# A decoder layer on one core: where the woven substitution steps stand beside VectorE's softmax operations

## The chip, the core and the metric

One core of a Trainium2 chip runs the whole kernel in one launch. The metric is the device time in microseconds (us) of one execution, as the median of several runs. The engines are TensorE (PE in the profile, its weight loads PEld), VectorE (DVE), ScalarE (ACT), GpSimd (POOL) and SyncE (SP, which issues most DMAs). Each has its own queue and works through it in order; they meet through semaphores.

## The reference

One layer over 2048 tokens of width 1024, all in float32. A normalised input goes through one projection into two groups of heads. Eight attention heads look back over a sliding window of 128 tokens, with a learned sink per head, whose logit takes part in the maximum and the sum of the softmax:

```python
s = s - slopes * dist                      # ALiBi
s = jnp.where(valid, s, NEG_INF)
m = jnp.maximum(jnp.max(s, axis=-1, keepdims=True), sink)
p = jnp.exp(s - m)
denom = jnp.sum(p, axis=-1, keepdims=True) + jnp.exp(sink - m)
o = einsum(p / denom, v)
```

Eight RWKV-7 heads update a 64x64 state per token; `S = S*w + (S a) b + v k`, read out as `S r`. Both groups share an output projection, and a gated MLP with a short causal convolution and a last normalisation follow.

## The kernel before

The first stage (to about 1150 us) does projection, attention and RWKV; then come the output projection and the MLP, which the change does not touch.

The first stage works in 16 units: four blocks of 512 tokens by four indices j, each with two RWKV heads and two attention heads. Loop `n` runs three units at once: projection and preparation of unit n+2, the chunk matrices of unit n+1, the recurrence (`chain`, eight chunks of 64 tokens) and the attention of unit n. The code issues instructions for all of them in one written order: a list `dense` of projection pieces, a list `other` of steps with positions from the table `Q`, and `defer`, which puts a step on a list to be issued some estimated microseconds later. `in_order` pins the order of TensorE, ScalarE and VectorE as issued; GpSimd's and SP's order is pinned in the prologue only.

For RWKV the inverse of a unit triangular matrix is needed per chunk. `px` makes the products, VectorE masks them into XB, `inv_in` sends the 32x32 diagonal blocks through DRAM (dL) and back as LL, laid out so that all blocks of a unit are solved at once on 128 partitions. `subst` is that forward substitution: 31 steps of two VectorE operations, `mul` (Mt = M x LL) and `add` (M = M + Mt), each needing the one before. `inv_out` sends M through DRAM (dT) to TT, and `merge0` (a transpose on VectorE) to `merge2` complete the inverse, which the next unit's `chain` needs.

The 62 operations of `subst` are not issued at once. They go onto the list `woven`. Each VectorE operation issued through `ordered` (line 120; its operations show as L124) calls `weave`, which issues one operation from the list behind it. `subst_to`, at 30 positions along the unit, issues what is still due by then, and `inv_out` stands behind the last.

Attention of a unit (`t_attn`) has four softmaxes, over q2 and g. `scores` issues the matmuls into pS and four VectorE operations: two fused reductions (the scaled scores plus bias, with the maximum into m; CUSTOM in the profile, each with a small read of its accumulator), the negation of m into nm, and es = nm + sink. `go1` follows later, with ScalarE's exponentials of es and P, which also sum; `go2` later still: sm + es, its reciprocal, and two scalings of P. `ptr` transposes P on TensorE, ScalarE copies it (pth), VectorE takes the rest (ptl), and `pv` multiplies by V into pO. In the profile the small operations show as m<-m, the scalings as P<-P. All of these VectorE operations go through `ordered`, so each is followed by a woven step while the list holds any.

Of the kernel before, what the change touches and what calls it, by code (L numbers as in the profile page):

```python
# [13 lines left out]
ALU = mybir.AluOpType  # L14
# [4 lines left out]
P = 128  # L19
# [64 lines left out]
def hybrid_trunk_kernel(  # L84
# [7 lines left out]
    order = {"on": True}  # L92
# [10 lines left out]
    def mm(**kw):  # L103
        in_order("pe", nc.tensor.matmul(**kw))  # L104

    def tr_(**kw):
        in_order("pe", nc.tensor.transpose(**kw))

    def act(*args, **kw):
        in_order("act", nc.scalar.activation(*args, **kw))  # L110
# [3 lines left out]
    def weave():  # L114
        if woven and not order.get("busy"):
            order["busy"] = True
            woven.pop(0)()
            order["busy"] = False

    def ordered(name):  # L120
        f = getattr(nc.vector, name)

        def go(*args, **kw):
            in_order("dve", f(*args, **kw))  # L124
            weave()
        return go
# [16 lines left out]
    tt = ordered("tensor_tensor")  # L143
    stt = ordered("scalar_tensor_tensor")
    tsc = ordered("tensor_scalar")
    vcopy = ordered("tensor_copy")
    recip = ordered("reciprocal")
    scan = ordered("tensor_tensor_scan")
    ttr = ordered("tensor_tensor_reduce")
# [3 lines left out]
    def f32(ap):  # L153
        return ap.bitcast(F32)
# [14 lines left out]
    def dma(**kw):  # L169
        i = nc.sync.dma_start(**kw)  # L170
        if order.get("prologue", True):
            in_order("sp", i)
# [16 lines left out]
    def mm3(ps, passes, first=True, last=True, **kw):  # L189
        n = len(passes)  # L190
        for i, (lh, ll, rh, rl) in enumerate(passes):
            mm(out=ps, lhsT=lh, rhs=rh, start=first and i == 0, stop=False, **kw)
            mm(out=ps, lhsT=lh, rhs=rl, start=False, stop=False, **kw)
            mm(out=ps, lhsT=ll, rhs=rh, start=False, stop=last and i == n - 1, **kw)


    with ExitStack() as A:
# [80 lines left out]
        sinkb = acon.tile([P, 8], F32, name="sinkb")  # L278
# [7 lines left out]
        bias = acon.tile([P, 256], mybir.dt.bfloat16, name="bias")  # L286
# [112 lines left out]
        def defer(us, fn, key=None):  # L399
            clk["n"] += 1  # L400
            todo.append((clk["t"] + us, clk["n"], fn, key))
            todo.sort(key=lambda d: d[:2])
# [6 lines left out]
        def need(key):  # L409
            while any(d[3] == key for d in todo):  # L410
                todo.pop(0)[2]()
# [328 lines left out]
        def t_x(F, n):  # L740
# [101 lines left out]
            def subst_to(i):  # L842
                def go():
                    while len(woven) > 2 * (30 - i):
                        weave()
                return go
# [152 lines left out]
        def t_attn(n):  # L999
            b, j = divmod(n, NPAIR)  # L1000
            S = {}

            def w0_(q2, e):
                return P if (b == 0 and q2 == 0 and e == 0) else 0

            def scores(q2, g):
                def go():
                    assert H["kb"] == b
                    need(f"q{j}_{b}")
                    need(f"kv_{b}")  # L1010
                    qg = H[b, j, "q"][g]
                    if q2 == 0 and g == 0:
                        S["o"] = ap_.tile([P, BLK], F32, tag="oT", name=f"oT_{b}_{j}")
                    u = f"{b}_{j}_{q2}_{g}"
                    hd = 4 * g + j
                    gs = hs[g]
                    Pm = S[q2, g] = ap_.tile([P, 2, 256], F32, tag="P", name=f"P_{u}", bufs=2)
                    col = ap_.tile([P, 4, 2], F32, tag="m", name=f"m_{u}", bufs=2)
                    m, nm, es, sm = (col[:, i] for i in range(4))
                    pS = ps_at.tile([P, 2, 256], F32, tag="at", name=f"pS_{u}")  # L1020
                    for e in range(2):
                        qb = 2 * q2 + e
                        w0 = w0_(q2, e)
                        kks = slice(qb + w0 // P, qb + 2)
                        qs = slice(qb * P, (qb + 1) * P)
                        mm(out=pS[:, e, w0:], lhsT=qg[:, qs], rhs=kTh[:, g, kks].rearrange("p n t -> p (n t)"),
                           start=True, stop=False)
                        mm(out=pS[:, e, w0:], lhsT=qg[:, qs], rhs=kTl[:, g, kks].rearrange("p n t -> p (n t)"),
                           start=False, stop=True)
                    for e in range(2):  # L1030
                        w0 = w0_(q2, e)
                        ttr(out=Pm[:, e, w0:], in0=pS[:, e, w0:], in1=bias[:, w0:],
                                                       scale=2.0 ** -(hd + 1), scalar=sinkb[:, hd:hd + 1], op0=ALU.add,
                                                       op1=ALU.max, accum_out=m[:, e:e + 1])
                    tsc(out=nm, in0=m, scalar1=-1.0, scalar2=None, op0=ALU.mult)
                    tt(out=es, in0=nm, in1=sinkb[:, hd:hd + 1].broadcast_to([P, 2]), op=ALU.add)

                    def go1():
                        act(es, es, AF.Exp)
                        for e in range(2):  # L1040
                            w0 = w0_(q2, e)
                            act(Pm[:, e, w0:], Pm[:, e, w0:], AF.Exp, bias=nm[:, e:e + 1], accum_out=sm[:, e:e + 1])
                        defer(Q["p2"], go2, f"p_{u}")

                    def go2():
                        tt(out=sm, in0=sm, in1=es, op=ALU.add)
                        recip(out=sm, in_=sm)
                        for e in range(2):
                            w0 = w0_(q2, e)
                            tsc(out=Pm[:, e, w0:], in0=Pm[:, e, w0:], scalar1=sm[:, e:e + 1], scalar2=None, op0=ALU.mult)  # L1050
                    defer(Q["p1"], go1, f"p_{u}")
                return go

            def ptr(q2, g):
                def go():
                    u = f"{b}_{j}_{q2}_{g}"
                    e0 = 1 if (b == 0 and q2 == 0) else 0
                    need(f"p_{u}")
                    need(f"p_{u}")
                    Pm = S[q2, g]  # L1060
                    pT = ps_at.tile([P, 4, P], F32, tag="at", name=f"pT_{u}")
                    for i in range(e0, 4):
                        tr_(out=pT[:, i], in_=Pm[:, i // 2, (i % 2) * P:(i % 2 + 1) * P], identity=ident)
                    th = S["th", g] = ap_.tile([P, 4, P], F32R, tag="pth", name=f"pth_{u}")
                    tl = S["tl", g] = ap_.tile([P, 4, P], F32R, tag="ptl", name=f"ptl_{u}")
                    act(th[:, e0:], pT[:, e0:], AF.Copy)
                    defer(Q["tl"], lambda: tt(out=tl[:, e0:], in0=pT[:, e0:], in1=f32(th[:, e0:]), op=ALU.subtract), f"t_{u}")
                return go

            def pv(q2, g):  # L1070
                def go():
                    u = f"{b}_{j}_{q2}_{g}"
                    e0 = 1 if (b == 0 and q2 == 0) else 0
                    assert H["vb"] == b
                    need(f"t_{u}")
                    th, tl = S["th", g], S["tl", g]
                    gs = hs[g]
                    pO = ps_at.tile([P, 2, P], F32, tag="at", name=f"pO_{u}")
                    for e in range(2):
                        qb = 2 * q2 + e  # L1080
                        mm3(pO[0:64, e], [(vth[:, qb + kb, gs], vtl[:, qb + kb, gs], th[:, 2 * e + kb], tl[:, 2 * e + kb])
                                          for kb in range(e0 if e == 0 else 0, 2)])
                    act(S["o"][gs, q2 * 256:(q2 + 1) * 256], pO[0:64].rearrange("p e q -> p (e q)"), AF.Copy)
                    if q2 == 1:
                        r0 = 64 * (4 * g + j)
                        dma(out=catT[r0:r0 + 64, b * BLK:(b + 1) * BLK], in_=S["o"][gs])
                return go

            return scores, ptr, pv
# [769 lines left out]
```

## Time and profile before

| | |
|---|---|
| median of 3 runs | 2682.14 us (2678.06 to 2682.83) |
| profiled execution | 2676.94 us |
| its span | 2675.2 us |
| busy: TensorE, VectorE, ScalarE, GpSimd | 94%, 65%, 49%, 55% |
| mean granted clock of TensorE | 0.976 |

The profile is that of one execution. Times in a timeline are from the start of its span. Busy time is what an engine's instructions took; a timeline's bracket gives idle time of the engine in front of an instruction and what released it. Durations on VectorE overlap a little: an instruction can start before the one in front of it has ended, so what a sequence costs is read from start to start.

### The profile page before, as it was taken

What the parts mean: (1) busy time and instruction counts of PE and PEld (TensorE: products, weight loads), DVE (VectorE), ACT (ScalarE), POOL (GpSimd) and SP (SyncE); (2) the same over time, 40 slices, a digit from 0 to 9 for tenths busy, and PEclk for the clock granted to TensorE, in tenths of its full rate; (3) what the DMA queues carried; (4) which work ended last, traced back from release to release, by engine and by line L of the source; (5) the groups of instructions that cost most, each with busy time, mean ns of one, the idle gap of its engine ahead of it and who ended that gap; (6) DMA issues with size and microseconds to landing.
All of it is one profiled execution on the core that took longest, in us unless ns stands there. A gap on an engine that the chain in (4) does not pass through costs nothing.

```text
span 2675.2 us, 42264 instructions
## 1 busy us (share of the span) xinstructions
PE 2524.3 (94%) x15211; PEld 1983.2 (74%) x15211; DVE 1733.0 (65%) x3216; ACT 1302.5 (49%) x2769; POOL 1469.3 (55%) x1364
## 2 busy tenths in 40 slices
PE   7899999999999989998989999999999999999997
PEld 5666666766667666777868787887888888888886
DVE  6578777777677746753757776767676765453336
ACT  4356655665556555544633433455333343343343
POOL 6434443444344433421747867767666665464598
PEclk9899999999999989999999999999999999999999
DMA  4222222222223222336664345455233336743354
GB/s 125 65 69 74 74 74 74 72 62 78 66 59 97 64 66 59 94 114 194 201 186 130 130 138 179 137 164 179 87 106 103 118 95 234 243 150 101 103 166 164
DMA packets 333108, 313.94 MB, mean 117 GB/s; under 512 B 102576, under 2 KB 254274, under 8 KB 332898
## 3 DMA queue, kind: packets, MB, share of 16 engines
q1 hardware_dynamic: 332290, 310.71, 38.3%
q8 instruction: 119, 1.95, 0.3%
q14 instruction: 91, 0.75, 0.1%
q10 hardware_dynamic: 608, 0.53, 0.1%
HBM read 229.26 MB, written 81.92 MB: 116 GB/s over the span
## 4 chain that ended last, share of the span: by engine, by line
PE 60%; DVE 18%; DMA 8%; ACT 5%; issue 4%; POOL 4%; SPq 1%; POOLq 0%; ACTq 0%; DVEq 0%
PE d L104 14%; PE q_g L104 13%; PE q_u L104 13%; DVE M L124 4%; DVE Mt L124 4%; PE pin_q L104 3%; DMA LL<-dL 3%; PE poa L104 2%; PE px L104 2%; PE po L104 2%; DVE P L124 2%; PE pc L104 2%; PE pin_k L104 1%; PE ph L104 1%; PE pO L104 1%
## 5 line engine op out<-in xcount | busy, mean ns | idle before, releaser
L1262 POOL TENSOR_TENSOR ul_u<-s_u,uh_u 128x512 fp32r<-128x512 f32 x154 | 214.2, 1398 | 144.3 <-ACT uh_u L110 141.1
L1262 POOL TENSOR_TENSOR ul_a<-sa,uh_a 128x512 fp32r<-128x512 f32 x154 | 210.3, 1373 | 139.7 <-ACT uh_a L110 137.7
L104 PE MATMUL q_u<-h2h,uh_u 128*128 128x512 f32 x616 | 241.3, 392 | 10.7 <-DVE u_u L1497 8.0
L1262 POOL TENSOR_TENSOR ul_g<-s_g,uh_g 128x512 fp32r<-128x512 f32 x154 | 215.9, 1410 | 59.8 <-ACT uh_g L110 57.8
L104 PE MATMUL q_g<-h2h,uh_g 128*128 128x512 f32 x616 | 241.3, 392 | 4.7 <-DVE u_g L1497 3.6
L104 PE MATMUL q_u<-h2h,ul_u 128*128 128x512 f32 x616 | 240.3, 390 | 0.4 <-POOL ul_u L1262 0.4
L104 PE MATMUL q_g<-h2l,uh_g 128*128 128x512 f32 x616 | 240.6, 391 | 0.0
L104 PE MATMUL q_g<-h2h,ul_g 128*128 128x512 f32 x616 | 240.3, 391 | 0.0
L104 PE MATMUL q_u<-h2l,uh_u 128*128 128x512 f32 x616 | 240.3, 390 | 0.0
L104 PE MATMUL d<-ul_b,uh_a 128*128 128x512 f32 x616 | 232.6, 390 | 1.8 <-DVE ul_b L1494 1.8
L104 PE MATMUL d<-uh_b,ul_a 128*128 128x512 f32 x616 | 229.4, 389 | 0.0
L110 ACT ACTIVATE uh_a<-sa 128x512 fp32r<-128x512 f32 x154 | 97.1, 631 | 228.3 <-PE d L104 127.6
L104 PE MATMUL d<-uh_b,uh_a 128*128 128x512 f32 x616 | 205.9, 389 | 0.0
L110 ACT ACTIVATE uh_u<-s_u 128x512 fp32r<-128x512 f32 x154 | 95.7, 628 | 208.9 <-DVE s_u L1494 93.7
L110 ACT ACTIVATE uh_g<-s_g 128x512 fp32r<-128x512 f32 x154 | 95.2, 629 | 207.5 <-PE q_u L104 112.7
L124 DVE TENSOR_TENSOR Mt<-M,LL 128x60 f32<-128x60 f32 (+24 forms) x496 | 159.1, 321 | 42.0 <-DMA LL<-dL 33.7
L1494 DVE TENSOR_TENSOR ul_b<-wd,uh_b 128x512 fp32r<-128x512 f32 x55 | 68.6, 1248 | 156.1 <-ACT uh_b L110 150.1
L124 DVE SCALAR_TENSOR_TENSOR cc<-g,fcst,cc 128x1024 f32<-128x1024 f32 x88 | 147.3, 1688 | 29.5 <-ACT cc L110 28.8
L124 DVE TENSOR_TENSOR M<-M,Mt 128x60 f32<-128x60 f32 (+24 forms) x496 | 156.2, 315 | 10.8
L104 PEld LDWEIGHTS q_u<-h2h,uh_u 128*128 128x128 f32 x616 | 116.0, 188 | 38.0 <-DVE u_u L1497 7.5
L104 PEld LDWEIGHTS q_g<-h2h,uh_g 128*128 128x128 f32 x616 | 116.3, 189 | 30.6 <-DVE u_g L1497 4.0
L104 PEld LDWEIGHTS d<-ul_b,uh_a 128*128 128x128 f32 x616 | 115.6, 188 | 27.2 <-DVE ul_b L1494 3.4
(371 smaller groups left out, 7014.0 us busy)
## 6 DMA issues: line engine op xcount, KB each, us to landing
sa<-actc SPq DMA_DIRECT2D x77, 512.0 KB
s_g<-in_ffn_w_gate_dram SPq DMA_DIRECT2D x44, 512.0 KB
s_u<-in_ffn_w_up_dram SPq DMA_DIRECT2D x44, 512.0 KB
actc<-cc SPq DMA_DIRECT2D x88, 256.0 KB
actc<-sa SPq DMA_DIRECT2D x66, 256.0 KB
wd<-in_ffn_w_down_dram SPq DMA_DIRECT2D x22, 512.0 KB
s_cat<-catT SPq DMA_DIRECT2D x20, 512.0 KB
x<-in_x_dram SPq DMA_DIRECT2D x16, 512.0 KB
```

The lines of the kernel that those rows point to most:

```text
L104: in_order("pe", nc.tensor.matmul(**kw))
L110: in_order("act", nc.scalar.activation(*args, **kw))
L124: in_order("dve", f(*args, **kw))
L1262: return nc.gpsimd.tensor_tensor(out=out, in0=in0, in1=in1, op=ALU.subtract)
L1494: return nc.vector.tensor_tensor(out=out, in0=in0, in1=in1, op=ALU.subtract)
```

## The change

A context `grouped(n)` holds weaving back while it is open and, when it closes, issues up to n woven operations. The four VectorE operations of `scores` go under `grouped(4)`, and so do the four of `go2`. The operations, their number and their order among themselves stay.

```diff
--- before.py
+++ after.py
@@ -116,6 +116,21 @@
             order["busy"] = True
             woven.pop(0)()
             order["busy"] = False
+
+    class grouped:
+
+
+        def __init__(self, n):
+            self.n = n
+
+        def __enter__(self):
+            self.was = order.get("busy")
+            order["busy"] = True
+
+        def __exit__(self, *exc):
+            order["busy"] = self.was
+            for _ in range(self.n):
+                weave()
 
     def ordered(name):
         f = getattr(nc.vector, name)
@@ -1027,13 +1042,14 @@
                            start=True, stop=False)
                         mm(out=pS[:, e, w0:], lhsT=qg[:, qs], rhs=kTl[:, g, kks].rearrange("p n t -> p (n t)"),
                            start=False, stop=True)
-                    for e in range(2):
-                        w0 = w0_(q2, e)
-                        ttr(out=Pm[:, e, w0:], in0=pS[:, e, w0:], in1=bias[:, w0:],
-                                                       scale=2.0 ** -(hd + 1), scalar=sinkb[:, hd:hd + 1], op0=ALU.add,
-                                                       op1=ALU.max, accum_out=m[:, e:e + 1])
-                    tsc(out=nm, in0=m, scalar1=-1.0, scalar2=None, op0=ALU.mult)
-                    tt(out=es, in0=nm, in1=sinkb[:, hd:hd + 1].broadcast_to([P, 2]), op=ALU.add)
+                    with grouped(4):
+                        for e in range(2):
+                            w0 = w0_(q2, e)
+                            ttr(out=Pm[:, e, w0:], in0=pS[:, e, w0:], in1=bias[:, w0:],
+                                                           scale=2.0 ** -(hd + 1), scalar=sinkb[:, hd:hd + 1], op0=ALU.add,
+                                                           op1=ALU.max, accum_out=m[:, e:e + 1])
+                        tsc(out=nm, in0=m, scalar1=-1.0, scalar2=None, op0=ALU.mult)
+                        tt(out=es, in0=nm, in1=sinkb[:, hd:hd + 1].broadcast_to([P, 2]), op=ALU.add)
 
                     def go1():
                         act(es, es, AF.Exp)
@@ -1043,11 +1059,12 @@
                         defer(Q["p2"], go2, f"p_{u}")
 
                     def go2():
-                        tt(out=sm, in0=sm, in1=es, op=ALU.add)
-                        recip(out=sm, in_=sm)
-                        for e in range(2):
-                            w0 = w0_(q2, e)
-                            tsc(out=Pm[:, e, w0:], in0=Pm[:, e, w0:], scalar1=sm[:, e:e + 1], scalar2=None, op0=ALU.mult)
+                        with grouped(4):
+                            tt(out=sm, in0=sm, in1=es, op=ALU.add)
+                            recip(out=sm, in_=sm)
+                            for e in range(2):
+                                w0 = w0_(q2, e)
+                                tsc(out=Pm[:, e, w0:], in0=Pm[:, e, w0:], scalar1=sm[:, e:e + 1], scalar2=None, op0=ALU.mult)
                     defer(Q["p1"], go1, f"p_{u}")
                 return go
```

## Rows read from the trace of the kernel before

**Rows 1.** The page: busy times, chain by engine, one group's costs

```profile
PE 2524.3 (94%) x15211; PEld 1983.2 (74%) x15211; DVE 1733.0 (65%) x3216; ACT 1302.5 (49%) x2769; POOL 1469.3 (55%) x1364
...
PE 60%; DVE 18%; DMA 8%; ACT 5%; issue 4%; POOL 4%; SPq 1%; POOLq 0%; ACTq 0%; DVEq 0%
...
L124 DVE TENSOR_TENSOR Mt<-M,LL 128x60 f32<-128x60 f32 (+24 forms) x496 | 159.1, 321 | 42.0 <-DMA LL<-dL 33.7
```

**Rows 2.** Sum of busy times over the fifteen stretches with softmax inside the substitution

```profile
sum 448.00, PE 408.70 PEld 289.59 DVE 411.66 ACT 252.84 POOL 168.16; mean PE 27.25 PEld 19.31 DVE 27.44 ACT 16.86 POOL 11.21
```

**Rows 3.** The chain of waits by line, 283 to 314 us

```profile
by line: DVE Mt L124 33.5%; DVE M L124 26.3%; DVE P L124 9.7%; DVE sw L124 7.4%; DVE m L124 5.4%; DVE hr L124 4.3%; DVE ptl L124 3.0%; issue 2.8%; DVE r L124 2.6%; DVE k L124 2.5%; DVE yo L124 2.2%; DVE bv L124 1.9%
```

**Rows 4.** VectorE's timeline, 421 to 429 us: start, duration, operation, [idle before <-releaser]

```profile
421.39 0.19 DVE L124 TENSOR_TENSOR Mt<-M,LL 128x31 f32<-128x31 f32 x1 [4.83 <-DMA LL<-dL]
...
422.23 0.15 DVE L124 TENSOR_TENSOR m<-m,sinkb 128x2 f32<-128x2 f32 x1
...
422.58 0.19 DVE L124 TENSOR_TENSOR Mt<-M,LL 128x29 f32<-128x29 f32 x1
422.80 0.19 DVE L124 TENSOR_TENSOR M<-M,Mt 128x29 f32<-128x29 f32 x1
...
423.85 0.15 DVE L124 TENSOR_TENSOR m<-m 128x2 f32<-128x2 f32 x1
...
424.73 0.35 DVE L124 TENSOR_SCALAR P<-P,m 128x256 f32<-128x256 f32 x1
424.99 0.21 DVE L124 TENSOR_TENSOR M<-M,Mt 128x50 f32<-128x50 f32 x1
425.23 0.21 DVE L124 TENSOR_TENSOR Mt<-M,LL 128x48 f32<-128x48 f32 x1
...
427.41 0.47 DVE L124 CUSTOM_DVE_ANT_0 P<-pS,bias,sinkb 128x256 f32<-128x256 f32 x1
...
428.75 0.16 DVE L124 TENSOR_TENSOR m<-m,sinkb 128x2 f32<-128x2 f32 x1
...
429.01 0.68 DVE L124 TENSOR_TENSOR ptl<-pT,pth 128x512 fp32r<-128x512 f32 x1
```

**Rows 5.** VectorE's timeline behind the substitution, 451 to 456 us

```profile
451.74 0.48 DVE L124 CUSTOM_DVE_ANT_0 P<-pS,bias,sinkb 128x256 f32<-128x256 f32 x1
...
452.86 0.16 DVE L124 TENSOR_TENSOR m<-m,sinkb 128x2 f32<-128x2 f32 x1
452.94 0.48 DVE L124 CUSTOM_DVE_ANT_0 P<-pS,bias,sinkb 128x256 f32<-128x256 f32 x1
...
454.28 0.16 DVE L124 TENSOR_TENSOR m<-m 128x2 f32<-128x2 f32 x1
...
454.68 0.62 DVE L124 TENSOR_SCALAR P<-P,m 128x256 f32<-128x256 f32 x2
455.21 0.75 DVE L124 SCALAR_TENSOR_TENSOR BK<-k,cst,BK 128x512 f32<-128x512 f32 x1
```

**Rows 6.** ScalarE's timeline at the late LL

```profile
422.42 0.20 ACT L110 ACTIVATE m<-m 128x2 f32<-128x2 f32 x1 [3.59 <-DVE m L124]
```

**Rows 7.** TensorE's timeline at the late LL

```profile
424.75 1.07 PE L107 MATMUL pT<-ident,P 128*128 128x128 f32 x4 [1.95 <-DVE P L124]
426.11 0.48 PE L104 MATMUL pc<-Pt,TT 64*64 64x64 f32 x4 [0.29 <-ACT Pt L110]
```

**Rows 8.** By stretch: length, busy PE, PEld, DVE, ACT, POOL; granted clock; DMA

```profile
425.10:431.90 6.80, 6.51 (x37) 4.53 (x36) 6.40 (x24) 5.54 (x16) 1.48 (x2) 0.50 0.00 1
...
981.50:995.20 13.70, 11.41 (x53) 7.98 (x55) 13.10 (x48) 10.71 (x29) 4.49 (x4) 0.50 0.01 3
456.00:465.00 9.00, 6.38 (x76) 4.54 (x74) 6.63 (x13) 3.53 (x11) 4.26 (x5) 1.00 0.49 130
```

**Rows 9.** VectorE's timeline, one step of the substitution at 311 us

```profile
311.51 1.23 DVE L124 TENSOR_TENSOR Mt<-M,LL 128x8 f32<-128x8 f32 x1
```

**Rows 10.** GpSimd's timeline at the same time

```profile
311.42 1.29 POOL L132 TENSOR_TENSOR am<-am,k 128x512 f32<-128x512 f32 x1
```

## The prediction

> **What bounds the kernel now.** I read the page first. TensorE is busy for 94% of the span, VectorE for 65%, and the chain that ended last lies on TensorE for 60% and on VectorE for 18% [rows 1]. Then I took the busy times by stretch. The change touches only the stretches in which substitution steps wait in the woven list while softmax runs. There are fifteen, one for each of sixteen units but the first, which has no attention beside it, between 147 and 1148 us. Of their 448 us VectorE is busy for 411.7 and TensorE for 408.7 [rows 2]: in these stretches, unlike over the span, VectorE is as full as TensorE. The chain of waits inside one of them, 283 to 314 us, lies on VectorE for most of its length, on M and Mt (the substitution) above all [rows 3]. So VectorE's time counts here; where it doesn't, TensorE's own work covers it.
>
> **What the change touches.** A softmax has two VectorE sequences: score (two fused add-max reductions, a negation, an addition) and normalise (an addition, a reciprocal, two scalings). There are 64 of each. In the VectorE timeline I counted those with woven steps between their operations: 31 and 31, from 147.5 us to 1146.5 us. In these 62 the four woven steps move behind the sequence. In the other 66 the list is empty and nothing changes. Nothing is added or removed, no DMA moves, and no wait is new. What changes is who stands beside whom on VectorE, and who stands behind a late LL.
>
> **Part 1: the order costs VectorE time.** A score sequence with steps between takes from 427.41 to 429.01, 1.60 us [rows 4]. One alone takes from 451.74 to 452.94, 1.20 us [rows 5], and four steps in a row, each on the result of the one before, start 0.22 us apart (422.58, 422.80 [rows 4]): 0.88. Together 2.08, so 0.48 us more. Normalise: 423.85 to 425.23, 1.38 us [rows 4], against 454.28 to 455.21, 0.93 [rows 5], and 0.88: 0.43 us more. The reason is in the same rows: the scaling at 424.73 lasts 0.35 us and the step behind it starts at 424.99, before it ends, as they share nothing; the step at 422.58 lasts 0.19 us and the next, which needs it, starts 0.03 us after its end. Woven steps filled such holes. Over 62 sequences that is 31 x 0.48 + 31 x 0.43 = 28 us of VectorE time.
> The Trainium skill, "VectorE: DVE Perf Modes", section "The DRAIN you can't avoid", says that the next operation doesn't start until the pipe has emptied, and that leaving out semaphores saves nothing. Taken alone, that makes order free and part 1 zero; the section sends the reader on for operations that are not held back, and these rows show them.
>
> **What each softmax gains.** The last score operation starts 1.34 us after the first when woven (427.41, 428.75), 1.12 when alone (451.74, 452.86): 0.22 us earlier. The second scaling ends 1.23 us after the sequence's start (424.73 + 0.35 - 423.85) against 1.02 (454.68 + 0.62 - 454.28): 0.21 us earlier [rows 4, 5]. The sequence gains half of what the engine loses behind it, and only the first of a stretch gets it whole.
>
> **How much of that reaches the end.** I followed the chain of waits through the fifteen stretches in order of time. On it lie 12 score and 17 normalise sequences with all their steps: 12 x 0.48 + 17 x 0.43 = 13.1 us. Five score and four normalise sequences are on it up to their last result, which then releases ScalarE or TensorE: 5 x 0.22 + 4 x 0.21 = 1.9 us gained. Four are of part 2. The other 20 are off it, most of them ahead of an idle time of VectorE that covers them; without that cover they would cost 20 x 0.46 = 9 us. Net: 11.2 us. Not all of it need stay. A multiplication of the substitution takes 0.2 us, yet 496 have a mean of 321 ns [rows 1]: some 0.11 x 496 = 55 us is waiting, and the additions do much the same. One such ran from 311.51 for 1.23 us [rows 9] and ended with GpSimd's operation of 311.42 for 1.29 us [rows 10]: VectorE stands until GpSimd is done. A VectorE that comes 0.5 us later to a run of such operations waits less, as far as ScalarE and not VectorE sets when GpSimd starts. The bounds are 0 and 11.2 us; I take half, 5.6, as these waits stand in most of the stretches but not all.
>
> **Part 2: the late LL.** In four stretches (from 147, 421, 700 and 980 us) the first step is woven behind the first of two score reductions and waits for the DMA of LL: 4.83 us at 421.39 [rows 4]. The second reduction, the negation and the addition stand behind it, so ScalarE sat idle for 3.59 us before the exponential [rows 6], and TensorE for 1.95 us before the transposes of P and again for 0.29 us for ScalarE's Pt [rows 7]. After the change the scores are done before the wait and the exponential runs under it. But the normalise sequence still stands behind the first ten steps, so behind the same LL. What it saves: the first four steps took until 422.58, 1.19 us, and alone take 0.88, so 0.31; its first scaling comes about 0.1 sooner, half of the 0.21; ScalarE's queue is ahead by then, so the 0.29 goes too. That is 0.7 us, four times: 2.8 us. What is late next is again normalise, behind LL.
> After that stall the clock was granted 0.50 (the 1.2 GHz level) for 6.8 us in which TensorE was busy for 6.51, and after the one at 980 us for 13.7 us with 11.41 busy [rows 8]. At the full level the same work takes half: 3.3 and 5.7 us less. Around 457 us TensorE also idled on normalise and 456 to 465 us stayed at 1.00 [rows 8], so a somewhat shorter stall may keep the clock. Ends: 0 and 9.0; I take 2, the first of the two at better than even, since the second stall stays long. Longer stalls elsewhere can lose the same.
>
> **Ends of the substitution.** In seven stretches the last steps are in a normalise sequence and move behind its second scaling, so M is complete, and the store to dT issued on SP, about 0.3 us later: 0 to 2 us. I take 0.5, since VectorE's transpose is often busy-bound then.
>
> **Sum.** +5.6 - 2.8 - 2 + 0.5 = +1.3 us. The profiled execution took 2676.94 us, 5.2 under the median of 2682.14; added to the median it gives 2683.4 us, which I call 2683. A measurement of this kernel can tell about 0.2%, 5.4 us, from no change. My forecast is no change that can be told, 0.42.
>
> **Rivals.**
> 1. Slower: VectorE's extra time is not swallowed. The place is the stretches from 283, 558 and 837 us, where the chain hardly leaves VectorE [rows 3] and all four sequences count: 0.48 + 3 x 0.43 = 1.8 us each. It decides as soon as GpSimd's operations move along with VectorE's. Then 11.2 - 2.8 + 0.5 = +8.9 us: 2691; with half the 20 covered ones out in the open too, 2696. Against it are the waits on GpSimd. 0.33.
> 2. Faster through the clock: ScalarE ahead by up to 3.6 us takes the edge off the four stalls and the low clock goes in full: 5.6 - 2.8 - 9.0 + 0.5 = -5.7, and without the 5.6, -11.3: 2671 to 2676. For it: the 0.50 rows follow these stalls. Against it: normalise still waits for LL. 0.19.
> 3. Order is free on VectorE: 0 - 2.8 - 1.9 - 2 = -6.7: 2675. The starts before an end [rows 4] speak against it. 0.06. The section of the Trainium skill named in part 1 would have it so.
> 4. The change doesn't do what it says, because the builder reorders: VectorE's order is pinned by hand, so hardly. GpSimd's and SP's isn't past the prologue and can shift by chance; that lies inside the range, with no share of its own.
>
> **How the numbers follow.** Same 0.42; slower 0.33 (rival 1); faster 0.25 (rivals 2 and 3). The range reaches from rival 2 to rival 1 with half of the covered sequences: 2671 to 2696. The likeliest case's own is 2677 to 2688.
>
> **What would show it.** Right: score sequences of 1.2 us everywhere; woven steps 0.22 us apart behind them; VectorE's busy time in the fifteen stretches not lower, their length up by 1 to 2 us where the chain is on VectorE; at 421 us the exponential ahead of LL and TensorE's wait for P about 1.5 us instead of 1.95. Wrong: transposes of P that no longer wait in those four stretches; fewer low-clock stretches; the fifteen stretches shorter; or time lost behind 1148 us, where nothing was touched.

## The result, and the profile after

The changed kernel takes 2694.30 us (median of 7 runs, 2688.50 to 2706.64) where the kernel before takes 2682.14: a ratio of 1.0063 with a 95% interval of 1.0044 to 1.0082, that is 16.9 us more (11.8 to 22.0). It is slower, and the interval leaves out no change at all. A second set of runs ("whole change" below) gave 1.0077 (1.0051 to 1.0103). The profiled execution of after took 2688.5 us (span 2686.8), the lowest of its runs and 11.6 over before's profiled 2676.94, so its trace shows only part of the loss.

The page of after: busy times, the chain by engine, and the two groups of the substitution (VectorE's helper is now line 139).

```profile
PE 2526.4 (94%) x15211; PEld 1983.8 (74%) x15211; DVE 1750.0 (65%) x3216; ACT 1302.5 (48%) x2769; POOL 1466.4 (55%) x1364
...
PE 59%; DVE 20%; DMA 8%; issue 4%; POOL 4%; ACT 4%; SPq 0%; POOLq 0%; ACTq 0%; DVEq 0%
...
L139 DVE TENSOR_TENSOR Mt<-M,LL 128x60 f32<-128x60 f32 (+24 forms) x496 | 158.1, 319 | 41.7 <-DMA LL<-dL 31.1
...
L139 DVE TENSOR_TENSOR M<-M,Mt 128x60 f32<-128x60 f32 (+24 forms) x496 | 149.6, 302 | 14.8
```

Against [rows 1], VectorE is busy 17 us longer with the same 3216 instructions, and the chain lies on it for 20% of the span instead of 18%. Where this happens shows in the fifteen stretches. Taken in both kernels from the first operation on Mt to the last on M, they sum like this in the trace of before:

```profile
sum 442.20, PE 402.91 PEld 285.96 DVE 407.56 ACT 248.63 POOL 164.63; mean PE 26.86 PEld 19.06 DVE 27.17 ACT 16.58 POOL 10.98
```

and like this in the trace of after:

```profile
sum 454.90, PE 408.54 PEld 290.70 DVE 420.22 ACT 236.18 POOL 165.01; mean PE 27.24 PEld 19.38 DVE 28.01 ACT 15.75 POOL 11.00
```

The stretches are 12.7 us longer (454.90 - 442.20), and VectorE's busy time in them is 12.7 us longer (420.22 - 407.56). Its idle time there was 34.6 us and is 34.7. But it is made up otherwise. The waits in it that a timeline brackets (over 0.15 us) fell from 17.1 us, 20 of them, to 6.9 us, 7 of them, while the short gaps between operations, such as those between dependent steps, grew from 17.6 us to 27.8. So some 10 us of waiting did give way. Between and before the stretches the trace of after lost nothing: its last operation on M ends 9.2 us later (1157.4 against 1148.2). The other 2.4 us of its loss come behind 1157 us, where nothing was changed.

VectorE's timeline of after, 428 to 435 us: a grouped normalise sequence with its four steps, then a grouped score sequence with its four.

```profile
428.92 0.15 DVE L139 TENSOR_TENSOR m<-m 128x2 f32<-128x2 f32 x1
429.11 0.17 DVE L139 RECIPROCAL m<-m 128x2 f32<-128x2 f32 x1
429.31 0.62 DVE L139 TENSOR_SCALAR P<-P,m 128x256 f32<-128x256 f32 x2
429.84 0.20 DVE L139 TENSOR_TENSOR Mt<-M,LL 128x52 f32<-128x52 f32 x1
430.08 0.21 DVE L139 TENSOR_TENSOR M<-M,Mt 128x52 f32<-128x52 f32 x1
430.32 0.21 DVE L139 TENSOR_TENSOR Mt<-M,LL 128x50 f32<-128x50 f32 x1
430.57 0.61 DVE L139 TENSOR_TENSOR M<-M,Mt 128x50 f32<-128x50 f32 x1
...
432.66 0.47 DVE L139 CUSTOM_DVE_ANT_0 P<-pS,bias,sinkb 128x256 f32<-128x256 f32 x1
...
433.78 0.16 DVE L139 TENSOR_TENSOR m<-m,sinkb 128x2 f32<-128x2 f32 x1
433.86 0.22 DVE L139 TENSOR_TENSOR Mt<-M,LL 128x66 f32<-128x66 f32 x1
434.11 0.23 DVE L139 TENSOR_TENSOR M<-M,Mt 128x66 f32<-128x66 f32 x1
434.38 0.23 DVE L139 TENSOR_TENSOR Mt<-M,LL 128x63 f32<-128x63 f32 x1
434.63 0.22 DVE L139 TENSOR_TENSOR M<-M,Mt 128x63 f32<-128x63 f32 x1
434.78 0.68 DVE L139 TENSOR_TENSOR ptl<-pT,pth 128x512 fp32r<-128x512 f32 x1
```

The bare sequences are as short as foretold: 0.92 us for normalise (428.92 to 429.84) and 1.20 for score (432.66 to 433.86). But the steps behind them start 0.24 to 0.27 us apart, not 0.22, so score with its four steps takes 2.12 us (432.66 to 434.78) against the 1.60 of [rows 4]. Over the 26 score and 30 normalise sequences that were woven in before and have all four steps, the median from the start to the operation behind the fourth step is 2.12 us for score, against 1.60 in before. For normalise it is 2.24 against 1.39. The lower quartile, where waits weigh least, is 2.07 against 1.55 and 1.90 against 1.37.

The late LL in the unit of 421 us, now 426.74. VectorE's timeline of after:

```profile
426.74 0.19 DVE L139 TENSOR_TENSOR Mt<-M,LL 128x31 f32<-128x31 f32 x1 [2.44 <-DMA LL<-dL]
```

ScalarE's timeline of after:

```profile
425.75 0.20 ACT L110 ACTIVATE m<-m 128x2 f32<-128x2 f32 x1
```

The exponential runs a microsecond ahead of LL, where it had waited 3.59 us [rows 6]. TensorE's stall of 1.95 us [rows 7] is gone there in this trace, and so is the low clock. In the unit of 980 us, now 991.7, TensorE's timeline of after still has this:

```profile
995.08 1.11 PE L107 MATMUL pT<-ident,P 128*128 128x128 f32 x4 [3.12 <-DVE P L139]
```

The windows of after at both places (length, busy PE, PEld, DVE, ACT, POOL, granted clock, DMA share, GB/s):

```profile
426.70:436.00 9.30, 8.47 (x68) 5.91 (x67) 8.54 (x37) 6.67 (x20) 0.62 (x1) 1.00 0.12 24
993.30:1000.10 6.80, 5.02 (x22) 3.64 (x22) 6.25 (x30) 2.51 (x8) 0.09 (x1) 0.50 0.01 4
```

Against [rows 8], 6.8 us at the 1.2 GHz level went at the first place, and at the second 6.8 are left of 13.7. So in this trace part 2 came about in part, and the time still rose.

The second trace of the same kernel ("whole change" below) has stall and low clock again at the first place. Its timelines of VectorE and of TensorE, and its window:

```profile
433.72 0.19 DVE L139 TENSOR_TENSOR Mt<-M,LL 128x31 f32<-128x31 f32 x1 [4.28 <-DMA LL<-dL]
...
437.04 0.83 PE L107 MATMUL pT<-ident,P 128*128 128x128 f32 x4 [2.20 <-DVE P L139]
...
437.50:447.70 10.20, 10.20 (x45) 7.07 (x44) 9.79 (x30) 6.84 (x17) 4.03 (x3) 0.50 0.00 1
```

There VectorE waited 4.28 us for LL behind the scores, where it had been 2.44, so what is gained at one place seems to hang on when LL lands. Around all four places together (from 5 us before the first Mt to 12 after it) TensorE idles for 8.8 us in before, 8.8 in after and 8.3 in the second trace; the low clock that goes with them is 23.9, 10.2 and 23.8 us. So a saving of part 2 in the whole change isn't shown.

### The profile page after: what moved, and what is told of

Same layout as the page of the kernel before. It is cut to its first block, busy times and chain, and to the rows that moved or that the text cites. A ratio compares the mean times of both kernels' runs of the same rounds, so it can differ in the third digit from the quotient of the medians.

```text
span 2686.8 us, 42267 instructions
## 1 busy us (share of the span) xinstructions
PE 2526.4 (94%) x15211; PEld 1983.8 (74%) x15211; DVE 1750.0 (65%) x3216; ACT 1302.5 (48%) x2769; POOL 1466.4 (55%) x1364
## 3 DMA queue, kind: packets, MB, share of 16 engines
q8 instruction: 119, 1.95, 0.3%
## 4 chain that ended last, share of the span: by engine, by line
PE 59%; DVE 20%; DMA 8%; issue 4%; POOL 4%; ACT 4%; SPq 0%; POOLq 0%; ACTq 0%; DVEq 0%
PE q_g L104 14%; PE d L104 14%; PE q_u L104 13%; DVE Mt L139 5%; DVE M L139 5%; DMA LL<-dL 3%; DVE P L139 3%; PE pin_q L104 2%; PE poa L104 2%; PE po L104 2%; PE px L104 2%; PE pc L104 2%; PE pin_k L104 1%; PE ph L104 1%; DVE m L139 1%
## 5 line engine op out<-in xcount | busy, mean ns | idle before, releaser
L139 DVE TENSOR_TENSOR M<-M,Mt 128x60 f32<-128x60 f32 (+24 forms) x496 | 149.6, 302 | 14.8
```

## Experiments

Each is timed against the kernel before on the same chip; a difference in us is the ratio less one, times that chip's median of before. Shortened diffs are against the changed kernel unless said otherwise. For partial groupings, `grouped(0)` leaves weaving as it was.

**One kind of sequence alone.** Scores grouped, normalise woven:

```diff
-                        with grouped(4):
+                        with grouped(0):
                             tt(out=sm, in0=sm, in1=es, op=ALU.add)
```

> Only the score sequences are grouped; normalise keeps its woven steps. Theory A (the dependent steps in a row cost VectorE 0.48 us a sequence, and this reaches the end): 31 x 0.48 = 15 us of VectorE time, minus what the late LL saves (3 to 5 us); with the whole change at +17 us, of which the late LL takes some -4, the two kinds cost about 21 us together, so scores some 11: about +6 to +8 us here. Rival B (the order of SP's and GpSimd's queues, which the builder chose differently, costs the time): this kernel's SP order differs from the one before in fewer places and not in those of the changed kernel, so 0 to +3 us or an odd value. Rival C (the late normalise results are what TensorE waits for, scores are harmless): -3 to 0 us.

Measured: 2689.27 against 2682.55 us, ratio 1.0030 (1.0012 to 1.0049), 8.0 us. And the other way round, scores woven:

```diff
-                    with grouped(4):
+                    with grouped(0):
                         for e in range(2):
```

> Only the normalise sequences are grouped; scores keep their woven steps, so the second score reduction still stands behind the late LL. Theory A: 31 x 0.43 = 13 us of VectorE time, half to three quarters of which reach the end: +8 to +11 us, and e1 and e2 add up to the whole change. Rival B (queue order): SP's order here is nearly that of the changed kernel, so all of +17 us. Rival C (normalise carries it all): +17 us too, but then e1 is not slower at all.

Measured: 2692.53 us, ratio 1.0035 (1.0016 to 1.0053), 9.4 us. The two halves cost about the same and add up to the whole (17.4 against 16.9). That bears on one side suspicion. The builder put the store M to dT behind other transfers on SP in several units of after; the normalise-only kernel has nearly the same order on SP (four lines differ) and costs half, so SP's order alone can't make up the whole.

**The four late score sequences alone.**

```diff
-                    with grouped(4):
+                    with grouped(4 if j == q2 == g == 0 else 0):
...
-                        with grouped(4):
+                        with grouped(0):
```

> Only the four score sequences that stand at the late LL are grouped (first of each block); everything else as before. Both SP's and GpSimd's orders stay. Theory A, part 2: 4 x 0.7 = 2.8 us saved and up to 9 us of low clock: -3 to -6 us, with ScalarE's exponential ahead of LL in those four stretches. Rival (normalise still behind LL, and what TensorE gains there it waits for later): within 1 us of the kernel before.

Measured: 2682.55 against 2682.55 us, ratio 0.9992 (0.9973 to 1.0012): 2.1 us less, between 7.2 less and 3.2 more. TensorE's timeline and window of this kernel at 980 us:

```profile
980.51 1.11 PE L107 MATMUL pT<-ident,P 128*128 128x128 f32 x4 [3.45 <-DVE P L140]
...
978.30:992.00 13.70, 11.49 (x55) 8.12 (x57) 13.37 (x48) 6.85 (x17) 4.11 (x4) 0.50 0.05 18
```

TensorE's idle time around 421 us shrinks from 2.24 us to 0.57 and around 700 us from 1.20 to 0.12, around 147 us it stays (1.21 and 1.63); the stall at 980, the longest, stays with its 13.7 us at the low clock, on P: normalise. The predicted 4.8 us (2.8 + 2) lie inside the interval, and so does nothing at all.

**The steps ahead of the sequence instead of behind it.** Same grouping, the four steps issued on entering:

```diff
+            for _ in range(self.n):
+                weave()
...
             order["busy"] = self.was
-            for _ in range(self.n):
-                weave()
```

> The four steps go in front of the grouped sequence, not behind. The holes between dependent steps are the same as in the changed kernel, but the substitution is not late by a softmax, the softmax is late by four steps instead (0.9 us), and all scores stand behind the late LL. Theory A (the holes): as slow as the changed kernel or slower, +17 to +25 us, VectorE's busy stretches as long. Rival D (the substitution's steps coming later is what costs): the steps come earlier here, so -5 to +5 us.

Measured: 2717.21 us, ratio 1.0118 (1.0084 to 1.0153), 31.7 us. That is more than the 17 to 25 expected. The loss isn't that the substitution comes late: with its steps early it is larger. Part of the extra is that all of softmax now stands behind the late LL: in this trace TensorE idles for 6.20 us at 1029 us, and its first stage (140 to 1160 us) has 129.7 us at the low clock, where that of before has 61.4. How the rest divides wasn't tried.

**The sequences that I had counted as covered, alone.** Twenty sequences, picked by block, unit and index:

```diff
+    some = set("v000 v001 v011 v031 v100 s101 v101 v111 s113 v112 v200 v211 s213 v212 v231 v300 s301 v301 s322 v322".split())
...
-                    with grouped(4):
+                    with grouped(4 if f"s{b}{j}{2 * q2 + g}" in some else 0):
```

> Grouped are only the 20 sequences (8 score... in all 20 of both kinds) that the prediction counted as off the chain and covered by an idle time of VectorE. The prediction's step: 0 to +2 us. Rival (there is no cover: VectorE's time in these stretches reaches the end wherever it is lost, at the 70% that e1 and e2 showed): 20 x 0.46 x 0.7 = +6.4 us.

Measured: 2687.41 against 2682.06 us, ratio 1.0036 (1.0012 to 1.0060): 9.7 us (3.2 to 16.1); the medians differ by 5.3. That is past the 0 to 2 us of the prediction.

**The 29 sequences on the chain with all their steps, alone.** The same edit with the other set.

> Grouped are only the 29 sequences (12 score, 17 normalise) that lie on the chain with all their steps. The prediction's step (half is swallowed by waits on GpSimd): +6.5 us. If nothing is swallowed: +13.1 us. If cost goes by number alone, as in e1 and e2: 29 x 0.45 x 0.7 = +9.2 us.

Measured: 2696.26 us, ratio 1.0059 (1.0036 to 1.0082): 15.8 us (9.7 to 22.0), where 13.1 had been their price and half of that what I kept. By the time nothing of it was swallowed, and they alone cost nearly as much as the whole change. The trace is less clear: the fifteen stretches are 9.5 us longer (451.70 against 442.20), and the first stage has 92.2 us at the low clock against 61.4 in before. So some of the 15.8 us may be the clock's.

**All but the covered ones, and the whole change beside it.** The set of the covered twenty with `not in some`:

> The changed kernel with 42 of its 62 sequences grouped: the 20 that I had counted as covered stay woven as in the kernel before. If these 20 truly have cover, this takes what the whole change takes, some 17 us over before (ratio 1.006), and the earlier run of the 20 alone (1.0036) was off to the high end of its interval. If they cost what that run says, 0.3 to 0.5 us each, this is 5 to 10 us faster than the whole change on the same chip: ratio 1.003 to 1.004.

> The changed kernel unaltered, beside the run above on the same chip, for that comparison. 1.004 to 1.008 over before, by its first measurement. If waits on GpSimd take up a steady part of the lost time, the substitution's 992 operations together are again busy for some 7 us less than in the kernel before (307.7 against 315.3 us the first time); if that was one execution's chance, the difference comes out near zero or with the other sign, as where only the scores or only the normalise sequences were grouped.

Measured on one chip: 2692.57 us, ratio 1.0059 (1.0037 to 1.0081), for the 42, and 2699.44 us, 1.0077 (1.0051 to 1.0103), for all 62. The twenty make a difference of 4.8 us by the ratios and 6.9 by the medians, but the intervals overlap. Beside the twenty alone (3.2 to 16.1) they probably cost something. But in that kernel's one trace the fifteen stretches grew by only 1.3 us (443.5 against 442.20), and VectorE's bracketed waits in them fell from 17.1 us to 6.9: the cover that the prediction counted on is there. So where their cost sits isn't shown. The 42 cost what the 29 of them cost, so the other 13 (those that release another engine, and the four late ones) cost nothing that can be told.

On the waits for GpSimd, the substitution's two groups in the second trace of the whole change:

```profile
L139 DVE TENSOR_TENSOR Mt<-M,LL 128x60 f32<-128x60 f32 (+24 forms) x496 | 160.2, 323 | 41.4 <-DMA LL<-dL 30.8
L139 DVE TENSOR_TENSOR M<-M,Mt 128x60 f32<-128x60 f32 (+24 forms) x496 | 148.0, 298 | 14.8
```

and with the scores alone grouped:

```profile
L140 DVE TENSOR_TENSOR Mt<-M,LL 128x60 f32<-128x60 f32 (+24 forms) x496 | 163.1, 329 | 45.4 <-DMA LL<-dL 36.1
...
L140 DVE TENSOR_TENSOR M<-M,Mt 128x60 f32<-128x60 f32 (+24 forms) x496 | 159.4, 321 | 12.6
```

In before they sum to 315.3 us (159.1 and 156.2). The whole change has 307.7 and 308.2, so it does wait some 7 us less inside these operations; the scores alone have 322.5 and normalise alone 320.8, more than before. The 29 sequences on the chain alone have 310.1, the 42 have 313.2. The relief is there in the whole change, is small, and doesn't come with every grouped sequence.

**The dependence taken away, woven and grouped.** In the kernel before and in the changed one the multiplication reads LL instead of M and the addition a constant instead of Mt, in the same shapes; the inverse is then not computed.

```diff
-                        tt(out=box["m"], in0=M[:, :m, i:i + 1].broadcast_to([P, m, w]),
+                        tt(out=box["m"], in0=LL[:, :m, i:i + 1].broadcast_to([P, m, w]),
...
-                        tt(out=M[:, :m, i + 1:], in0=M[:, :m, i + 1:], in1=box["m"], op=ALU.add)
+                        other = cent[:, :m * (31 - i)].rearrange("p (k t) -> p k t", k=m)
+                        tt(out=M[:, :m, i + 1:], in0=M[:, :m, i + 1:], in1=other, op=ALU.add)
```

> The kernel before, with the substitution's dependence taken out: the multiplication reads LL in place of M, the addition reads a constant in place of Mt (the inverse is not computed), so that no step needs the one in front of it; the order is that of before, softmax woven. Theory A: steps in a row start about 0.12 us apart and not 0.22 to 0.25; with some 600 such neighbours VectorE has 60 us less to do in the stage, and the kernel is 20 to 40 us faster than before. If order costs for another reason (issue, semaphores), steps still start 0.2 us apart and the time stays.

> The changed kernel with the same dependence taken out (the inverse is not computed). Theory A: a score sequence with four free steps behind takes 1.20 + 4 x 0.12 = 1.68 against 1.60 us, normalise 1.41 against 1.38, so 31 x 0.08 + 31 x 0.03 = 3.4 us of VectorE time are left, and the late LL gives 2 to 3 us back: within 3 us of e8. If the place of the steps and not their dependence costs, the distance to e8 stays at +17 us.

Measured: woven 2621.12 us, ratio 0.9788 (0.9760 to 0.9816), 57 us less where 20 to 40 had been expected; grouped 2621.26 us, 0.9779 (0.9753 to 0.9804). VectorE's timeline of the grouped one, the steps behind a score sequence:

```profile
412.57 0.47 DVE L139 CUSTOM_DVE_ANT_0 P<-pS,bias,sinkb 128x256 f32<-128x256 f32 x1
...
413.77 0.22 DVE L139 TENSOR_TENSOR Mt<-LL 128x66 f32<-128x66 f32 x1
413.91 0.22 DVE L139 TENSOR_TENSOR M<-M,cent 128x66 f32<-128x66 f32 x1
414.05 0.22 DVE L139 TENSOR_TENSOR Mt<-LL 128x63 f32<-128x63 f32 x1
414.18 0.22 DVE L139 TENSOR_TENSOR M<-M,cent 128x63 f32<-128x63 f32 x1
414.32 0.68 DVE L139 TENSOR_TENSOR ptl<-pT,pth 128x512 fp32r<-128x512 f32 x1
```

These are the operations shown above from 433.86 on, equally long (0.22 us), but 0.14 us apart instead of 0.25. The four take 0.55 us (413.77 to 414.32) instead of 0.92 (433.86 to 434.78). Grouping still costs VectorE something: the median score sequence with its steps is 1.75 us here and 1.50 in the woven one, 0.25 more instead of 0.52, where 0.08 had been expected; I put that down to the holes inside softmax itself. And yet the two kernels take the same time. The sum over the stretches says why. Woven and free:

```profile
sum 395.30, PE 372.96 PEld 265.14 DVE 346.26 ACT 246.20 POOL 159.72; mean PE 24.86 PEld 17.68 DVE 23.08 ACT 16.41 POOL 10.65
```

Grouped and free:

```profile
sum 390.50, PE 373.95 PEld 266.97 DVE 349.78 ACT 232.48 POOL 156.06; mean PE 24.93 PEld 17.80 DVE 23.32 ACT 15.50 POOL 10.40
```

TensorE is busy for 94 to 96% of these stretches (372.96 of 395.30, 373.95 of 390.50) and VectorE for 88 to 90, where it was TensorE 91 and VectorE 92 before. With VectorE no longer what the stretch waits for, 0.25 us a sequence is covered: its bracketed waits in the stretches are 48.2 us in the woven one and 36.2 in the grouped one, where before had 17.1. So the change costs time for two reasons together: dependent steps stand in a row, and the engine on which they do is the bound. Freeing the steps takes away both at once, so these runs don't say what either would cost alone.

**Substitution begun later in the units with the late LL.** This starts from the kernel before, nothing is grouped. The first step goes behind the first normalise sequence:

```diff
             SB0, SB1, TS, M1, M2 = Q["sub"]
+            if an % NPAIR == 0 and an >= 0:
+                SB0 = 8.2
```

> Nothing is grouped here. In the four units that begin a block the substitution's first step goes from position 6.5 to 8.2 of the unit, so that the first score sequence and the first normalise sequence both stand ahead of the wait for LL on VectorE. Theory (what is late next behind LL is normalise, and both are worth time): the stalls of TensorE at 147, 421, 700 and 980 us (1.15, 2.24, 0.54 and 4.19 us of idle time in the kernel before) go nearly all, some 7 us, and the low clock behind them, 24 us at half speed in the trace of before, goes in part, 0 to 10 us; the steps that the substitution has lost in between are made up, as its end is set by the wait for GpSimd and not by its start: 8 to 12 us faster, 2670 to 2675. Rival (the substitution's end is what counts): M comes some 1.5 us later in four units and the next unit's chain waits for it: the two cancel, within 4 us of before, 2678 to 2686. Rival (the late LL is hidden by TensorE's own work whatever stands behind it, as the late steps alone moved nothing that could be told): within 2 us of before.

And with 7.4 in place of 8.2:

> The same edit with position 7.4: between the first score sequence and the first normalise sequence of those four units, so that the scores stand ahead of the wait for LL and the normalise sequence stands where the plan puts it. If normalise is what counts, this gives less than position 8.2: the stall at 980 us (4.19 us idle, 13.7 us at the low clock) stays as it did where the four score sequences alone were grouped, and the time is within 4 us of before, 2678 to 2686. If any later start serves, it gives what 8.2 gives or more, since it delays M by half as much: 2670 to 2677.

Measured on one chip: 2674.95 us and 2676.09 us against 2685.28; ratios 0.9972 (0.9950 to 0.9993) and 0.9970 (0.9947 to 0.9994), 7.5 and 8.1 us. Both are a little faster than before, and so than the changed kernel. VectorE's timeline of the first, at 980 us:

```profile
985.65 0.62 DVE L124 TENSOR_SCALAR P<-P,m 128x256 f32<-128x256 f32 x2
987.21 0.19 DVE L124 TENSOR_TENSOR Mt<-M,LL 128x31 f32<-128x31 f32 x1 [0.95 <-DMA LL<-dL]
```

TensorE's timeline and the window there:

```profile
987.91 0.66 PE L107 MATMUL pT<-ident,P 128*128 128x128 f32 x4
...
984.00:997.70 13.70, 13.17 (x108) 9.52 (x108) 11.02 (x37) 11.55 (x33) 4.46 (x4) 1.00 0.17 29
```

The scalings are done 0.9 us before LL arrives, the transposes don't wait, and the clock stays full. Around the four places TensorE idles for 8.8 us in before, 5.8 with the late scores alone grouped and 1.5 here; the low clock that goes with them falls from 23.9 us over 17.1 to none. That bears out the theory for the stalls, at the lower end of its 8 to 12 us (7.5 by the ratio, 10.3 by the medians). Over the whole first stage (140 to 1160 us) this one trace has no less low clock, 64.9 us against 61.4. The second kernel falls out of its expectation: normalise still stands behind LL there, but behind four woven steps instead of ten, TensorE idles for 5.1 us at the four places with 3.4 us of low clock, and no difference to the first can be told. So a later start serves, and that normalise stands behind LL at all isn't by itself what costs.

**The clock over whole runs.** Each run lists TensorE's mean granted clock. On the same chip its median is 0.973 for before and 0.970 for the whole change; 0.973 and 0.9705 for the 29 sequences; 0.973 and 0.9715 for the twenty; 0.973 and 0.982 for the free woven kernel; 0.971 and 0.9745 for the first step later. Over the 82 runs of before that stand beside the experiments, 0.01 less goes with some 21 us more (a straight line through them, so an estimate). By it the clock carries some 6 of the 20.6 us of the whole change, 5 of the 15.8, 3 of the 9.7, 19 of the 57, and as good as all of the 7.5. Whether the changed order lowers the clock through the waits that it makes, or how else, wasn't tried.

## Why the prediction was wrong

The forecast was 2683 us, no change that can be told; it came out slower, at 2694.30, as in the first rival and a little above its 2691. The range to 2696 holds it, but that it lands near the first rival is in part luck: that sum is too low on the order's cost and takes off 2.8 us for the late LL, which the whole change doesn't show.

**What the change touches: 62 right, 31 and 31 wrong.** In the trace of before 26 score and 36 normalise sequences have woven steps between their operations. The sum stays, 26 x 0.48 + 36 x 0.43 = 28 us; the expectations of the first two experiments carry the same error. Nor is it so that no DMA moves: the builder changed SP's order, which rival 4 allowed for.

**Part 1, the order costs VectorE time: right, a little small.** The mechanism is the one read from [rows 4, 5], and freeing the steps shows it: a step on the result of the one before starts after that one's end, an independent one before. The size was 0.48 and 0.43 us; the lower quartiles show 0.52 (2.07 - 1.55) and 0.53 (1.90 - 1.37), because I had priced the four steps by 128x29 (0.22 us apart), and those behind most sequences are 128x48 to 128x76 (0.24 to 0.27). That is some 33 us of VectorE time over 62 sequences instead of 28.

**What each softmax gains: seen, without effect at the end.** Scores and scalings are done earlier, as the bare sequences show; the 13 sequences that release another engine or wait for LL change nothing that can be told (42 cost what 29 do).

**How much of that reaches the end: the step that failed,** at the half that the waits on GpSimd were to swallow. The 29 sequences on the chain cost 15.8 us (9.7 to 22.0), which holds all of their 13.1 and not 6.5. I had taken the 55 us of waiting inside the steps as room for a later VectorE. The measured relief there is 7 us in the whole change and none in either part. With the 10 us of bracketed waits that gave way, some 18 of the 33 us of VectorE time were made up in the trace of after, and 12.7 us of longer stretches were left (16.6 in the second trace), where the forecast left 5.6. So the step was mis-sized: less of the waiting could be won back than I counted. How much of the 15.8 us is VectorE's and how much the lower clock stays open. The other half of the step, the 20 covered sequences at nothing, stays open as well: alone they cost 9.7 us by the time, of which the clock may be 3, but their trace shows the cover. Rival 1 had this as its upper end.

**Part 2, the late LL: the right places, too little shown.** At 980 us normalise was late next, as foretold. At 421 us stall and low clock went in one trace of the whole change and not in the other, and over the four places TensorE idled as long as before. By the four late scores alone it is worth 2.1 us, predicted 4.8, and the measurement can tell neither from zero. The later start shows that there are 7 to 8 us to be had at these four places.

**Rival 2, the clock,** didn't come: over the first stage (140 to 1160 us) there are 61.4 us at the low level in the trace of before and 58.0 in after, and in the second trace of the whole change 105.8. If anything the clock went the other way, which the forecast names in one sentence (stalls elsewhere) and gives no price. **Rival 3, order is free on VectorE,** falls. The Trainium skill, "VectorE: DVE Perf Modes", section "The DRAIN you can't avoid", holds a next operation until the pipe is empty, and adds that one that isn't held starts earlier; here an independent step starts 0.08 us before the end of a 0.22 us one, and a dependent one 0.03 us behind it, and that difference is what the change paid for. **Ends of the substitution** (0.5 us; the trace of before has six such stretches, not seven) stay unmeasured by themselves.

The sum as measured: 15.8 us for 29 sequences, nothing for 13, 1 to 10 for 20; the whole gave 16.9 and 20.6.

## What to carry to other kernels

Two independent chains of small operations on one engine are worth more interleaved than one after the other: each fills the other's holes. Before such an order is changed, price it from start to start in the stretch where that engine is the bound, with the shapes that really stand there, and let it count in full where the chain lies on the engine. It is made up only as far as there is waiting left on that engine: here 17.1 us of bracketed waits in before against some 33 us of loss, and 48.2 with the steps freed, where the loss (0.25 us a sequence, some 15 us) came out nowhere. Look at the clock beside the time, over all runs and not in one trace. For a late input, start the work that needs it behind the work that doesn't, rather than regroup everything.

## What the runs showed of the hardware

The holes of the substitution are dear: the same 992 operations in the same shapes, without the dependence, take 57 us off the kernel (ratio 0.9788), although they are busy for only 23 us less (150.2 and 142.1 against 159.1 and 156.2). Part of the rest is the time from start to start (0.14 us between neighbours instead of 0.25), and part is the clock: in the first stage 34.1 us at the low level against 61.4.

How long the low clock lasts isn't read off the stall in front of it. 3.94 us of idle TensorE at 983 us (before) and 3.45 (late scores) were followed by 13.7 us at 0.50, 3.12 (after) by 6.8; in the second trace of the whole change 2.20 us were followed by 10.2, and in the kernel with position 7.4 2.23 us by 3.4. A stall of 1.63 us at 711 us in after had none behind it. What else decides was not tried.
